# adaLN pieces on VectorE handed out one behind each weight tile's low part, one modulation back on TensorE, one moved into the last SwiGLU

## The chip, the core and the metric

The kernel runs on one core of a Trainium2 chip. Its time is device microseconds (us) of one execution. TensorE (PE in the profile, with its weight loads as PEld) does the matrix products, VectorE (DVE) and ScalarE (ACT) the elementwise work, GpSimd (POOL) a little of it, and SyncE (SP) issues the transfers. Each engine works through its own queue in order and waits there on semaphores.

## What is computed

Two layers over 256 latent and 256 context tokens of width 1024. Every sub-layer is modulated by nine vectors per layer, which come from the conditioning vector by one large product with `w_ada` (the adaLN modulations, number 0 to 8):

```python
m_x = jnp.split((jax.nn.silu(c) @ w_ada[l] + b_ada[l])[:, None, :], N_MOD, axis=-1)
m_c = jnp.split((jax.nn.silu(c_ctx) @ w_ada[l] + b_ada[l])[None, None, :], N_MOD, axis=-1)
x = post_norm(x, 0.5 * m_x[2] * swiglu(modulate(x, m_x[0], m_x[1]), ffn1_wi[l], ffn1_wo[l]), ln_g[l, 0], ln_b[l, 0])
# the same for ctx, then the mixer with m[3..5], then ffn2 with m[6..8]
def swiglu(u, wi, wo):
    gate, up = jnp.split(u @ wi, 2, axis=-1)
    return (jax.nn.silu(gate) * up) @ wo
```

So a layer is SwiGLU (ffn1), mixer, SwiGLU (ffn2). In the last layer ffn2 works on the 256 latent tokens alone.

## The kernel before

**The four SwiGLUs.** `ffn` is called four times; they are called A (layer 0, ffn1), B (layer 0, ffn2), C (layer 1, ffn1) and D (layer 1, ffn2, latent tokens only) below. Each has a first part, the product with `wi`, and a second with `wo`. The first part runs over 22 column blocks m. A block has two weight tiles of 128x1024, gate and up. For each, `wload` issues a 512 KB transfer on SP into `raw` (3 buffers), ScalarE writes the high part `whi` (line 256) and VectorE the low part `wlo` (line 257; 2 buffers of each). `gemm` then runs 24 matmuls a tile, 8 times the three products of lines 266 to 268, the third of which reads `wlo`. After a block, `swiglu` forms `sg` on ScalarE and VectorE (line 420) and splits it into `hh` (ScalarE) and `hl` (VectorE, line 273). In A, B and C the first two blocks run in halves of the tokens while the layer norm ahead of them is ending; block 2 is the first that runs whole.

**The modulations on VectorE.** `ada_pieces` makes one modulation out of nine closures. Eight are pieces: a 512 KB transfer of 128 rows of `w_ada` into `araw` (2 buffers), and two VectorE instructions over 128x1024 that add it, times one column of the conditioning, to the two accumulators (line 192 for the first piece, line 194 for the others). The ninth, the close, sums over the partitions on TensorE (line 199), copies with ScalarE (line 202), transposes on TensorE (line 206) and adds the bias on VectorE (line 208). The accumulators `acc` hold two modulations and have one buffer; the residual `z` of the second part uses the same memory.

**How they are handed out.** `whole` fills the list `bgq` ahead of each `ffn`: six modulations in A, five in B, five in C, none in D. `ffn` traces `nbg` = 3 closures after each block (and after each of the four half blocks at the start), and what is left at the end of the first part. A scheduler then puts the instructions of each engine in an order by its own estimate of when they are ready, so the position in the code sets the order only roughly.

**The modulations on TensorE.** `ada_blocks` makes modulations 0 and 1 of layer 0 at the start of the kernel: for a piece, a 512 KB transfer and four matmuls of 32x256 side by side (line 150); at the end a VectorE copy of the row sums (line 154) and small matmuls with `sel` (line 159).

Of the kernel before, what the change touches and what calls it, by code (L numbers as in the profile page):

```python
# [7 lines left out]
F32 = mybir.dt.float32  # L8
F32R = mybir.dt.float32r
AF = mybir.ActivationFunctionType  # L10
ALU = mybir.AluOpType
# [3 lines left out]
P = 128  # L15
D = 1024
# [5 lines left out]
KF = 22  # L22
# [13 lines left out]
LAT = slice(0, SEQ)  # L36
CTXS = slice(SEQ, NT)
FULL = slice(0, NT)
HALVES = [LAT, CTXS]
# [15 lines left out]
class Program:  # L55
    def __init__(self, tc, A):
        self.tc = tc
        self.nc = tc.nc
        self.A = A
        self.bgq = []  # L60


    def setup(self, ctx):
# [151 lines left out]
    def bg(self, n):  # L215
        while n > 0 and self.bgq:
            self.bgq.pop(0)()
            n -= 1

    def bg_all(self):  # L220
        self.bg(len(self.bgq))

# [20 lines left out]
    def wload(self, src, n, hold=None):  # L243


        nc = self.nc
        raw = self.wp.tile([P, 1024], F32, tag="raw", name="raw", bufs=3)
        nc.sync.dma_start(out=raw[:, :n], in_=src)
        if hold is None:
            hold = [[self.wp.tile([P, 1024], F32R, tag=t, name=t) for t in ("whi", "wlo")]]  # L250
        whs, wls = [], []
        w = 1024 // len(hold)
        for i, (hi, lo) in enumerate(hold):
            r = raw[:, w * i:min(w * i + w, n)]
            m = r.shape[1]
            nc.scalar.activation(out=hi[:, :m], in_=r, func=AF.Copy)  # L256
            nc.vector.tensor_tensor(out=lo[:, :m], in0=r, in1=hi[:, :m].bitcast(F32), op=ALU.subtract)  # L257
            whs += [hi[:, P * k:P * k + P] for k in range(m // P)]
            wls += [lo[:, P * k:P * k + P] for k in range(m // P)]
        return whs, wls  # L260
# [124 lines left out]

        self.ready = [self.wload(s, 1024) for s in srcs]

    def ffn(self, l, which, halves, nxt_fn, nbg, final=None, then=()):
        nc = self.nc
        wi, wo = self.A[which + "_wi"][l], self.A[which + "_wo"][l]  # L390
        ln, gi = (0, 2) if which == "ffn1" else (2, 8)
        self.bd = 0 if which == "ffn1" else 2
        full = slice(halves[0].start, halves[-1].stop)
        with ExitStack() as ctx:
            self.tmp = ctx.enter_context(self.tc.tile_pool(name=f"ft{l}{which}", bufs=2))
            self.abufs = 2
            self.zp = ctx.enter_context(self.tc.tile_pool(name=f"fz{l}{which}", bufs=1))
            self.acc = None
            hp = ctx.enter_context(self.tc.tile_pool(name=f"fh{l}{which}", bufs=KF))
            self.psum(ctx, f"f{l}{which}", mm=6)  # L400
            hh, hl = [], []
            two = len(halves) == 2

            def load(m, held=False):
                ws = []
                for i in range(2):
                    hold = None
                    if held and m > 0:
                        hold = [[hp.tile([P, NT], F32R, tag=t, name="w" + t) for t in ("hh", "hl")] for _ in range(2)]
                    ws.append(self.wload(wi[m, i], 1024, hold=hold))  # L410
                return ws

            def wi_gemm(ps, ws, h):
                for p, w in zip(ps, ws):
                    self.gemm(p[:, h], w, [t[:, h] for t in self.uh], [t[:, h] for t in self.ul])

            def swiglu(pg, pu):
                sg = self.tmp.tile([P, NT], F32, tag="sg", name="sg")
                nc.scalar.activation(out=sg[:, full], in_=pg[:, full], func=AF.Silu)
                nc.vector.tensor_tensor(out=sg[:, full], in0=pu[:, full], in1=sg[:, full], op=ALU.mult)  # L420
                a = hp.tile([P, NT], F32R, tag="hh", name="hh")
                b = hp.tile([P, NT], F32R, tag="hl", name="hl")
                self.split(a[:, full], b[:, full], sg[:, full])
                hh.append(a)
                hl.append(b)

            def banks():
                return [self.bank("mm", [P, NT], n) for n in ("ps_fg", "ps_fu")]


            early = 2 if two else 0
            ps = [banks() for _ in range(early)]
            ready, self.ready = self.ready, []
            ws = [m == 0 and ready or load(m, True) for m in range(early)]
            for h in halves if two else []:
                for m in range(early):
                    wi_gemm(ps[m], ws[m], h)
                    self.bg(nbg)
            for p in ps:
                swiglu(*p)  # L440
            for m in range(early, KF):
                p = banks()
                wi_gemm(p, m == 0 and ready or load(m), full)
                swiglu(*p)
                self.bg(nbg)
            self.bg_all()
            gate = self.gate(l, gi)
            nxt = nxt_fn()
            dst = self.norm_dst(l, ln, nxt, final)
            zt = self.zp.tile([P, KD, NT], F32, tag="z", name="z", bufs=1)  # L450
            self.z = [zt[:, k, :] for k in range(KD)]
            pts = {}

            def wo_gemm(m, h):
                pt = pts[m]
                for a, b in ((0, 8), (8, 15), (15, 22)):
                    w = self.wload(wo[m, :, a:b].rearrange("p k c -> p (k c)"), (b - a) * P)
                    self.gemm(pt[:, h], w, [t[:, h] for t in hh[a:b]], [t[:, h] for t in hl[a:b]], a == 0, b == KF)

            late = 1 if two else 0  # L460
            for m in range(KD):
                pts[m] = self.bank("mm", [P, NT], "ps_o")
                if m < KD - late:
                    xr = self.load_x(m, full)
                    wo_gemm(m, full)
                    for h in halves:
                        self.residual(m, pts[m], xr, h, gate)
                        self.stats_add(m, h)
            for h in halves:
                for m in range(KD - late, KD):  # L470
                    xr = self.load_x(m, h)
                    wo_gemm(m, h)
                    res = self.residual(m, pts[m], xr, h, gate)
                    self.stats_add(m, h)
                if h is not halves[0]:
                    self.ln_norm(l, ln, halves[0], nxt, dst, bc, res)
                if h is halves[-1]:
                    self.make_ready(*then)
                bc = self.ln_stats(h)
            self.ln_norm(l, ln, h, nxt, dst, bc)  # L480
            self.xsrc = dst
# [838 lines left out]
    def whole(self, out):  # L1320
        def wi(l, which):
            return [self.A[which + "_wi"][l, 0, i] for i in range(2)]

        self.start(wi(0, "ffn1"))
        for l in range(DEPTH):
            last = l == DEPTH - 1
            for i in ([2, 3, 4, 5, 6, 7] if l == 0 else [4, 5, 6, 7, 8]):
                self.bgq += self.ada_pieces(l, i)
            self.ffn(l, "ffn1", HALVES, lambda: self.mod_next(l, 3, (l, 0)), 3,
                     then=[self.A["w_in"][l, t] for t in (T_WD, T_AD)])  # L1330
            self.mixer(l, not last, lambda: self.mod_next(l, 6, (l, 1)), wi(l, "ffn2"))
            if not last:
                self.bgq += self.ada_pieces(l, 8)
                for i in range(4):
                    self.bgq += self.ada_pieces(l + 1, i)
                self.ffn(l, "ffn2", HALVES, lambda: self.mod_next(l + 1, 0, (l, 2)), 3, then=wi(l + 1, "ffn1"))
            else:
                self.ffn(l, "ffn2", [LAT], lambda: None, 0, final=out)


def pack(I):
    import numpy as np
    f = np.float32
    A = {}
    xt = np.concatenate([I["x"][0], I["ctx"][0]], 0)
    A["xT"] = xt.T.reshape(KD, P, NT)
    A["cvec"] = np.stack([I["c"][0], I["c_ctx"]], 1).reshape(KD, P, 2).transpose(1, 0, 2)
    A["w_ada0"] = I["w_ada"][0, :, 0:2 * D].reshape(2, 4, P, 2, 4, 256).transpose(3, 4, 0, 2, 1, 5)
    A["w_ada"] = I["w_ada"].reshape(DEPTH, KD, P, 9, D).transpose(0, 3, 1, 2, 4)
    A["bada"] = I["b_ada"].reshape(DEPTH, 9, KD, P).transpose(3, 0, 1, 2)  # L1350
    A["lngb"] = np.stack([I["ln_g"], I["ln_b"]], 2).reshape(DEPTH, 3, 2, KD, P).transpose(4, 0, 1, 2, 3)
# [31 lines left out]
    r = np.arange(SEQ) // GRID_W  # L1383
# [19 lines left out]
    i = np.arange(C)  # L1403
# [30 lines left out]
```

## Time and profile before

| what | value |
|---|---|
| median of 3 runs | 2971.82 us (2965.13 to 2972.13) |
| the profiled execution, its own time | 2964.87 us |
| its span | 2963.1 us |
| busy: PE, PEld, DVE, ACT, POOL | 2806.9, 2237.2, 1779.9, 1069.1, 278.9 us |
| mean granted TensorE clock | 0.965 of full speed |
| VectorE instructions of line 194 (pieces) | 224, 277.2 us |
| DMA, mean over the span | 127 GB/s |

The profiled execution lies 6.95 us under the median and at the low end of the runs; between its span and its time lie 1.8 us. Busy time of PE is modelled: a matmul's record is longer than the distance to the next one, so the distance between starts is what a matmul costs. The granted clock is a share of full speed, and takes one of two levels, 1.2 or 2.4 GHz, at a time. A line in the profile is that of the kernel before, and can be a helper's.

### The profile page before, as it was taken

The page shows a single profiled execution, that of the slowest core. Times are in us where ns is not written, and L with a number is a line of the kernel's source. Part 1 is how long each engine was busy: PE and PEld are TensorE (multiplying, and loading weights), DVE is VectorE, ACT ScalarE, POOL GpSimd, SP SyncE. Part 2 cuts the span into 40 slices and gives each one's busy share as a digit, 9 for nine tenths or more (in the row PEclk, how much of TensorE's full clock was granted, in tenths as well). Part 3 has the DMA queues.
Part 4 walks back from the last instruction along what each step waited for, and adds up shares of the span by engine and source line. Part 5 has one row for each costly group of instructions (what it writes and reads, how often), then busy time and mean ns, then how long its engine had stood idle before and what let it go on. Part 6 is the DMA issues. An engine that isn't in the chain of part 4 may idle for free. (4 is left out here: it accounts for less than half of the span.)

```text
span 2963.1 us, 48510 instructions
## 1 busy us (share of the span) xinstructions
PE 2806.9 (95%) x19598; PEld 2237.2 (76%) x19598; DVE 1779.9 (60%) x3039; ACT 1069.1 (36%) x1929; POOL 278.9 (9%) x274
## 2 busy tenths in 40 slices
PE   7999999999999899998999998999999999898998
PEld 5788887666666776696788876788876677777998
DVE  5983346756674357659832478532568786476554
ACT  3223134323232246442222332222543433364543
POOL 0000011100000111220000110001210100022000
PEclk8999999999999999999999998999999998899998
DMA  7763343221122433346623366433432223354454
GB/s 274 232 221 99 108 137 96 76 68 45 43 59 71 149 104 109 111 139 219 199 94 107 116 206 208 143 97 114 152 107 80 60 64 102 110 138 138 159 179 147
DMA packets 205313, 376.61 MB, mean 127 GB/s; under 512 B 79776, under 2 KB 109088, under 8 KB 205088
## 3 DMA queue, kind: packets, MB, share of 16 engines
q1 hardware_dynamic: 205088, 373.51, 40.7%
q8 instruction: 154, 2.52, 0.3%
q14 instruction: 71, 0.58, 0.1%
HBM read 340.93 MB, written 31.46 MB: 126 GB/s over the span
## 5 line engine op out<-in xcount | busy, mean ns | idle before, releaser
L256 ACT ACTIVATE whi<-raw 128x1024 fp32r<-128x1024 f32 (+1 forms) x399 | 415.2, 1041 | 1072.5 <-PE ps_o L267 305.7
L257 DVE TENSOR_TENSOR wlo<-raw,whi 128x1024 fp32r<-128x1024 f32 (+1 forms) x399 | 500.3, 1255 | 416.5 <-ACT whi L256 410.8
L194 DVE SCALAR_TENSOR_TENSOR acc<-araw,cs,acc 128x1024 f32<-128x1024 f32 x224 | 277.2, 1279 | 28.1 <-DMA araw<-in_w_ada 27.1
L266 PE MATMUL ps_o<-hh,whi 128*128 128x512 f32 (+1 forms) x770 | 270.5, 351 | 0.0
L268 PE MATMUL ps_o<-hh,wlo 128*128 128x512 f32 (+1 forms) x770 | 267.3, 347 | 0.0
L266 PE MATMUL ps_fg<-uh,whi 128*128 128x512 f32 (+1 forms) x704 | 256.8, 365 | 10.2 <-ACT whi L256 6.5
L267 PE MATMUL ps_o<-hl,whi 128*128 128x512 f32 (+1 forms) x770 | 265.5, 345 | 0.0
L268 PE MATMUL ps_fg<-uh,wlo 128*128 128x512 f32 (+1 forms) x704 | 255.2, 362 | 8.5 <-DVE wlo L257 8.5
L268 PE MATMUL ps_fu<-uh,wlo 128*128 128x512 f32 (+1 forms) x704 | 255.3, 363 | 8.2 <-DVE wlo L257 8.2
L762 PE MATMUL ps_gate<-uh,whi 128*128 128x512 f32 (+1 forms) x672 | 255.3, 380 | 3.1 <-ACT whi L256 3.1
L266 PE MATMUL ps_fu<-uh,whi 128*128 128x512 f32 (+1 forms) x704 | 253.8, 361 | 3.1 <-ACT whi L256 3.1
L763 PE MATMUL ps_gate<-ul,whi 128*128 128x512 f32 (+1 forms) x672 | 255.4, 380 | 0.0
L764 PE MATMUL ps_gate<-uh,wlo 128*128 128x512 f32 (+1 forms) x672 | 254.0, 378 | 0.7 <-DVE wlo L257 0.5
L267 PE MATMUL ps_fg<-ul,whi 128*128 128x512 f32 (+1 forms) x704 | 254.4, 361 | 0.1
L267 PE MATMUL ps_fu<-ul,whi 128*128 128x512 f32 (+1 forms) x704 | 253.7, 360 | 0.0
L266 PEld LDWEIGHTS ps_fg<-uh,whi 128*128 128x128 f32 x704 | 135.7, 193 | 39.8 <-ACT whi L256 15.2
L268 PEld LDWEIGHTS ps_o<-hh,wlo 128*128 128x128 f32 x770 | 144.6, 188 | 20.3
L267 PEld LDWEIGHTS ps_o<-hl,whi 128*128 128x128 f32 x770 | 144.5, 188 | 19.6
L268 PEld LDWEIGHTS ps_fg<-uh,wlo 128*128 128x128 f32 x704 | 135.6, 193 | 30.3 <-DVE wlo L257 10.7
L268 PEld LDWEIGHTS ps_fu<-uh,wlo 128*128 128x128 f32 x704 | 135.7, 193 | 30.2 <-DVE wlo L257 11.1
L266 PEld LDWEIGHTS ps_o<-hh,whi 128*128 128x128 f32 x770 | 144.8, 188 | 17.4
L266 PEld LDWEIGHTS ps_fu<-uh,whi 128*128 128x128 f32 x704 | 135.7, 193 | 24.4 <-ACT whi L256 5.6
(298 smaller groups left out, 5268.3 us busy)
## 6 DMA issues: line engine op xcount, KB each, us to landing
raw<-in_ffn_wi SPq DMA_DIRECT2D x176, 512.0 KB, 3.9
araw<-in_w_ada SPq DMA_DIRECT2D x144, 512.0 KB, 4.3
raw<-in_w_in SPq DMA_DIRECT2D x92, 512.0 KB, 3.6
raw<-in_ffn_wo SPq DMA_DIRECT2D x70, 448.0 KB, 3.3
raw<-in_ffn_wo SPq DMA_DIRECT2D x35, 512.0 KB, 3.5
pd<-fg SPq DMA_DIRECT2D x52, 256.0 KB, 2.0
raw<-in_w_branch SPq DMA_DIRECT2D x24, 512.0 KB, 3.7
praw<-in_w_in SPq DMA_DIRECT2D x44, 256.0 KB, 2.8
```

The lines of the kernel that those rows point to most:

```text
L194: nc.vector.scalar_tensor_tensor(out=a, in0=raw, scalar=c, in1=a, op0=ALU.mult, op1=ALU.add)
L256: nc.scalar.activation(out=hi[:, :m], in_=r, func=AF.Copy)
L257: nc.vector.tensor_tensor(out=lo[:, :m], in0=r, in1=hi[:, :m].bitcast(F32), op=ALU.subtract)
L266: nc.tensor.matmul(pt, wh, xh[k], start=first and k == 0, stop=False)
L267: nc.tensor.matmul(pt, wh, xl[k], start=False, stop=False)
L268: nc.tensor.matmul(pt, wl, xh[k], start=False, stop=last and k == n - 1)
L762: nc.tensor.matmul(pt, wh, xh, start=k == 0, stop=False)
L763: nc.tensor.matmul(pt, wh, xl, start=False, stop=False)
L764: nc.tensor.matmul(pt, wl, xh, start=False, stop=k == KD - 1)
```

## The change

Four things. A new method `bg_after` traces closures under `issue_after(self.lo.ins)`: each VectorE instruction among them gets an edge that keeps it behind the last `wlo` instruction in VectorE's queue. `load` calls it with one closure after each weight tile (`every` = 1: after each; 4: after every fourth), and the two half blocks of the context tokens hand out one each; the old three closures after a block are gone. Modulation 2 of layer 0 goes to `ada_blocks`, in eight pieces, one at the end of each of the blocks 2 to 9 of A. Modulation 8 of layer 1 moves from C to D, one closure after every fourth tile.

```diff
+    def bg_after(self, n):
+        with self.tc.issue_after(self.lo.ins):
+            self.bg(n)
...
-            nc.vector.tensor_tensor(out=lo[:, :m], in0=r, in1=hi[:, :m].bitcast(F32), op=ALU.subtract)
+            self.lo = nc.vector.tensor_tensor(out=lo[:, :m], in0=r, in1=hi[:, :m].bitcast(F32), op=ALU.subtract)
...
+            slots = iter(range(2 * KF))
...
                     ws.append(self.wload(wi[m, i], 1024, hold=hold))
+                    if next(slots) % every == 0:
+                        self.bg_after(1)
...
                     wi_gemm(ps[m], ws[m], h)
-                    self.bg(nbg)
+                    if h.start:
+                        self.bg_after(1)
...
                 swiglu(*p)
-                self.bg(nbg)
+                if self.bgpe:
+                    self.bgpe.pop(0)()
...
-            for i in ([2, 3, 4, 5, 6, 7] if l == 0 else [4, 5, 6, 7, 8]):
+            for i in ([3, 4, 5, 6, 7] if l == 0 else [4, 5, 6, 7]):
                 self.bgq += self.ada_pieces(l, i)
-            self.ffn(l, "ffn1", HALVES, lambda: self.mod_next(l, 3, (l, 0)), 3,
+            if l == 0:
+                self.new_mod(0, 2)
+                self.bgpe = self.ada_blocks(0, [2], 0, 4)
+            self.ffn(l, "ffn1", HALVES, lambda: self.mod_next(l, 3, (l, 0)), 1,
...
-                self.ffn(l, "ffn2", [LAT], lambda: None, 0, final=out)
+                self.bgq += self.ada_pieces(l, 8)
+                self.ffn(l, "ffn2", [LAT], lambda: None, 4, final=out)
```

The arrays change in one place: `w_ada0`, the copy of the weights that `ada_blocks` reads, holds three modulations in place of two. New line numbers: pieces 193 and 195, close 200, 203, 207 and 209, `wlo` 263, `sg` 429, `hl` 279, TensorE's pieces 151, row copy 155, `sel` matmuls 160. Outside of the four SwiGLUs no engine's order changes.

**Place 1: VectorE in B, blocks 3 to 5.** Before, from the `sg` of block 2 on (`wlo_11920` is the up tile of block 3, `wlo_12004` and `wlo_12010` are the tiles of block 4):

```order
L420 TENSOR_TENSOR sg_11890<-ps_fu_11829,sg_11890 128x512
L257 TENSOR_TENSOR wlo_11920<-raw_11917,whi_11919 128x1024
L194 SCALAR_TENSOR_TENSOR acc_11614<-araw_11733,cs_71,acc_11614 128x1024 x2
L194 SCALAR_TENSOR_TENSOR acc_11614<-araw_11737,cs_71,acc_11614 128x1024 x2
L273 TENSOR_TENSOR hl_11894<-sg_11890,hh_11893 128x512
L420 TENSOR_TENSOR sg_11971<-ps_fu_11910,sg_11971 128x512
L192 TENSOR_SCALAR acc_11614<-araw_11802,cs_71 128x1024 x2
L208 TENSOR_TENSOR mod0_8_11523<-ps_ada2_11747,c_bada_74 128x8 x2
L273 TENSOR_TENSOR hl_11975<-sg_11971,hh_11974 128x512
L194 SCALAR_TENSOR_TENSOR acc_11614<-araw_11806,cs_71,acc_11614 128x1024 x2
L257 TENSOR_TENSOR wlo_12004<-raw_12001,whi_12003 128x1024
L194 SCALAR_TENSOR_TENSOR acc_11614<-araw_11810,cs_71,acc_11614 128x1024 x2
```

Now, from the same `sg` on (`wlo_11889` is the up tile of block 3, `wlo_11956` and `wlo_11975` are those of block 4):

```order
L429 TENSOR_TENSOR sg_11867<-ps_fu_11798,sg_11867 128x512
L263 TENSOR_TENSOR wlo_11889<-raw_11886,whi_11888 128x1024
L195 SCALAR_TENSOR_TENSOR acc_11566<-araw_11882,cs_71,acc_11566 128x1024
L279 TENSOR_TENSOR hl_11871<-sg_11867,hh_11870 128x512
L195 SCALAR_TENSOR_TENSOR acc_11566<-araw_11882,cs_71,acc_11566 128x1024
L195 SCALAR_TENSOR_TENSOR acc_11566<-araw_11892,cs_71,acc_11566 128x1024 x2
L429 TENSOR_TENSOR sg_11944<-ps_fu_11875,sg_11944 128x512
L263 TENSOR_TENSOR wlo_11956<-raw_11953,whi_11955 128x1024
L279 TENSOR_TENSOR hl_11948<-sg_11944,hh_11947 128x512
L263 TENSOR_TENSOR wlo_11975<-raw_11972,whi_11974 128x1024
L209 TENSOR_TENSOR mod0_8_11533<-ps_ada2_11965,c_bada_74 128x8 x2
L193 TENSOR_SCALAR acc_11566<-araw_11978,cs_71 128x1024 x2
```

Between the up tile of block 3 and the gate tile of block 4 stood four pieces (one of them a first piece), two `hl` and an `sg`; now two pieces, an `hl` and an `sg` stand there.

**Place 2: VectorE in D, one block in the steady part.** Before (gate tile, `sg` of the block ahead, up tile, `hl`):

```order
L257 TENSOR_TENSOR wlo_24928<-raw_24925,whi_24927 128x1024
L420 TENSOR_TENSOR sg_24916<-ps_fu_24855,sg_24916 128x256
L257 TENSOR_TENSOR wlo_24934<-raw_24931,whi_24933 128x1024
L273 TENSOR_TENSOR hl_24920<-sg_24916,hh_24919 128x256
L257 TENSOR_TENSOR wlo_24997<-raw_24994,whi_24996 128x1024
```

Now, in the seven blocks that have a piece so (the other blocks are as before):

```order
L263 TENSOR_TENSOR wlo_24970<-raw_24967,whi_24969 128x1024
L195 SCALAR_TENSOR_TENSOR acc_24690<-araw_24973,cs_71,acc_24690 128x1024
L429 TENSOR_TENSOR sg_24958<-ps_fu_24897,sg_24958 128x256
L195 SCALAR_TENSOR_TENSOR acc_24690<-araw_24973,cs_71,acc_24690 128x1024
L279 TENSOR_TENSOR hl_24962<-sg_24958,hh_24961 128x256
L263 TENSOR_TENSOR wlo_24980<-raw_24977,whi_24979 128x1024
```

The two instructions of a piece stand on both sides of `sg`, and the up tile's `wlo` has moved behind the second and behind `hl`.

**Place 3: TensorE in A, from a block's last matmul into the next.** Before, at a close:

```order
L268 MATMUL ps_fu_1233<-uh_93,wlo_1243 128x512
L199 MATMUL ps_ada_1309<-acc_888,one_82 32x512 x4
L266 MATMUL ps_fg_1322<-uh_86,whi_1326 128x512
L267 MATMUL ps_fg_1322<-ul_94,whi_1326 128x512
L268 MATMUL ps_fg_1322<-uh_86,wlo_1327 128x512
L266 MATMUL ps_fg_1322<-uh_87,whi_1326 128x512
L267 MATMUL ps_fg_1322<-ul_95,whi_1326 128x512
L206 MATMUL ps_ada2_1315<-c_ident_78,acc_888 128x128 x4
L268 MATMUL ps_fg_1322<-uh_87,wlo_1327 128x512
```

Now, at the end of block 9, with the last piece of modulation 2 and its `sel` matmuls, four matmuls later (`rows_1289` is VectorE's copy, which stands behind the `sg` of block 9 there):

```order
L274 MATMUL ps_fu_1206<-uh_93,wlo_1221 128x512
L151 MATMUL ps_ada_682<-araw_1283,cs_71 32x256 x4
L272 MATMUL ps_fg_1295<-uh_86,whi_1299 128x512
L273 MATMUL ps_fg_1295<-ul_94,whi_1299 128x512
L274 MATMUL ps_fg_1295<-uh_86,wlo_1300 128x512
L272 MATMUL ps_fg_1295<-uh_87,whi_1299 128x512
L160 MATMUL ps_ada2_1291<-c_sel_69,rows_1289 128x8 x2
L273 MATMUL ps_fg_1295<-ul_95,whi_1299 128x512
```

Each of the eight pieces (`L151`, four matmuls) stands so between two blocks, and `L160` waits on VectorE in the midst of block 10.

## Rows read from the trace of the kernel before

**Rows 1.** The page's second part: busy tenths of VectorE in 40 slices.

```profile
DVE  5983346756674357659832478532568786476554
```

**Rows 2.** Waits of TensorE over the whole span: total us, times, longest.

```profile
PE ps_fg L268 <- DVE wlo L257: 8.5, 6, 5.5
PE ps_fu L268 <- DVE wlo L257: 8.2, 4, 3.9
```

**Rows 3.** Ten microseconds of B: window, length, busy of PE, PEld, DVE, ACT, POOL, clock, DMA.

```profile
1350.00:1360.00 10.00, 4.11 (x22) 2.01 (x21) 9.00 (x13) 2.17 (x3) 0.00 (x0) 0.86 0.57 166
```

**Rows 4.** VectorE's order of time, B without pieces: start, us, instruction, idle before.

```profile
1486.58 0.69 DVE L420 TENSOR_TENSOR sg<-ps_fu,sg 128x512 f32<-128x512 f32 x1 [3.37 <-PE ps_fu L268]
1497.46 0.69 DVE L420 TENSOR_TENSOR sg<-ps_fu,sg 128x512 f32<-128x512 f32 x1 [3.37 <-PE ps_fu L268]
```

**Rows 5.** TensorE's order of time: first matmul of block 2, first behind block 21.

```profile
64.00 0.40 PE L266 MATMUL ps_fg<-uh,whi 128*128 128x512 f32 x1
...
300.52 0.40 PE L266 MATMUL ps_o<-hh,whi 128*128 128x512 f32 x1
...
1326.87 0.40 PE L266 MATMUL ps_fg<-uh,whi 128*128 128x512 f32 x1
...
1573.35 0.40 PE L266 MATMUL ps_o<-hh,whi 128*128 128x512 f32 x1
...
1734.39 0.40 PE L266 MATMUL ps_fg<-uh,whi 128*128 128x512 f32 x1
...
1982.25 0.40 PE L266 MATMUL ps_o<-hh,whi 128*128 128x512 f32 x1
```

**Rows 6.** TensorE's order of time at a close in A.

```profile
130.30 0.39 PE L268 MATMUL ps_fu<-uh,wlo 128*128 128x512 f32 x1
130.62 1.07 PE L199 MATMUL ps_ada<-acc,one 128*32 128x512 f32 x8
...
133.01 0.48 PE L267 MATMUL ps_fg<-ul,whi 128*128 128x512 f32 x1
```

**Rows 7.** VectorE, then TensorE, in B at blocks 3 and 4; TensorE in C.

```profile
1346.94 4.87 DVE L194 SCALAR_TENSOR_TENSOR acc<-araw,cs,acc 128x1024 f32<-128x1024 f32 x4 [0.74 <-DMA araw<-in_w_ada]
...
1358.58 1.22 DVE L257 TENSOR_TENSOR wlo<-raw,whi 128x1024 fp32r<-128x1024 f32 x1
...
1351.91 1.06 PE L199 MATMUL ps_ada<-acc,one 128*32 128x512 f32 x8 [0.34 <-issue]
...
1359.85 0.79 PE L268 MATMUL ps_fg<-uh,wlo 128*128 128x512 f32 x1 [5.51 <-DVE wlo L257]
...
1759.37 0.50 PE L268 MATMUL ps_fg<-uh,wlo 128*128 128x512 f32 x1 [1.23 <-DVE wlo L257]
```

**Rows 8.** The tile `araw`: a piece's instruction (ns), and its transfer (us to landing).

```profile
L194 DVE SCALAR_TENSOR_TENSOR acc<-araw,cs,acc x224: 1272/1279/1287, 49.1 to 1880.1; 128x1024 f32<-128x1024 f32 x112
...
DMA to landing us min/median/max: 3.4/4.3/10.0
```

**Rows 9.** TensorE's order of time at the kernel's start (modulations 0 and 1).

```profile
9.82 1.08 PE L150 MATMUL ps_ada<-araw,cs 128*32 128x256 f32 x8 [0.20 <-DMA araw<-in_w_ada]
...
20.46 0.61 PE L159 MATMUL ps_ada<-c_sel,rows 128*128 128x8 f32 x4 [1.60 <-DVE rows L154]
...
21.87 3.26 PE L150 MATMUL ps_ada<-araw,cs 128*32 128x256 f32 x32
```

**Rows 10.** VectorE, then TensorE, in one block of D.

```profile
2840.10 1.23 DVE L257 TENSOR_TENSOR wlo<-raw,whi 128x1024 fp32r<-128x1024 f32 x1 [1.37 <-ACT whi L256]
2842.03 0.42 DVE L420 TENSOR_TENSOR sg<-ps_fu,sg 128x256 f32<-128x256 f32 x1 [0.70 <-PE ps_fu L268]
2842.93 1.23 DVE L257 TENSOR_TENSOR wlo<-raw,whi 128x1024 fp32r<-128x1024 f32 x1 [0.47 <-ACT whi L256]
...
2845.86 1.22 DVE L257 TENSOR_TENSOR wlo<-raw,whi 128x1024 fp32r<-128x1024 f32 x1 [1.37 <-ACT whi L256]
...
2844.88 0.28 PE L268 MATMUL ps_fu<-uh,wlo 128*128 128x256 f32 x1
```

More of the change, by code (lines that the diff above doesn't have):

```diff
@@ L60, in __init__ @@
         self.bgq = []
+        self.bgpe = []
     def setup(self, ctx):
@@ L386, in make_ready, with ffn @@
         self.ready = [self.wload(s, 1024) for s in srcs]
-    def ffn(self, l, which, halves, nxt_fn, nbg, final=None, then=()):
+    def ffn(self, l, which, halves, nxt_fn, every, final=None, then=()):
         nc = self.nc
@@ L1335, in whole @@
                     self.bgq += self.ada_pieces(l + 1, i)
-                self.ffn(l, "ffn2", HALVES, lambda: self.mod_next(l + 1, 0, (l, 2)), 3, then=wi(l + 1, "ffn1"))
+                self.ffn(l, "ffn2", HALVES, lambda: self.mod_next(l + 1, 0, (l, 2)), 1, then=wi(l + 1, "ffn1"))
             else:
-                self.ffn(l, "ffn2", [LAT], lambda: None, 0, final=out)
+                self.bgq += self.ada_pieces(l, 8)
+                self.ffn(l, "ffn2", [LAT], lambda: None, 4, final=out)
 def pack(I):
@@ L1347, in pack @@
     A["cvec"] = np.stack([I["c"][0], I["c_ctx"]], 1).reshape(KD, P, 2).transpose(1, 0, 2)
-    A["w_ada0"] = I["w_ada"][0, :, 0:2 * D].reshape(2, 4, P, 2, 4, 256).transpose(3, 4, 0, 2, 1, 5)
+    A["w_ada0"] = I["w_ada"][0, :, 0:3 * D].reshape(2, 4, P, 3, 4, 256).transpose(3, 4, 0, 2, 1, 5)
     A["w_ada"] = I["w_ada"].reshape(DEPTH, KD, P, 9, D).transpose(0, 3, 1, 2, 4)
```

## The prediction

> **What bounds the kernel now.** I read the page's slices first, then the waits of TensorE, then the order of time of TensorE and VectorE in each SwiGLU. The slices say where VectorE is full: its nines stand where the pieces are handed out, most of all in B and C [rows 1], although over the whole span it is not the busiest engine. The waits say who suffers: TensorE waits for `wlo`, ten times, 16.7 us in all [rows 2]. That is less than what is lost, because the granted clock falls behind a long wait: in the ten microseconds of B around the wait of 5.51 us TensorE is busy for 4.11 us and has a mean clock of 0.86, while VectorE works for 9.00 [rows 3, 7]. Of the two levels, 1.2 and 2.4 GHz, part of that window ran at the lower.
>
> To size the whole loss I compare the length of 20 blocks (2 to 21) with what they take when nothing is in the way. In B behind the last piece two `sg` of neighbouring blocks stand 1497.46 − 1486.58 = 10.88 us apart, with TensorE the releaser and VectorE idle for 3.37 us [rows 4], so 20 blocks at full speed are 217.6. They took 236.5 in A, 246.5 in B and 247.9 in C [rows 5]. A close costs TensorE the distance between the matmuls around it less five spacings: (133.01 − 130.30) − 5 × 0.227 = 1.58 us [rows 6]. With six, five and five closes the losses are 236.5 − 217.6 − 9.5 = 9.4 in A, 246.5 − 217.6 − 7.9 = 21.0 in B and 22.4 in C. Some 53 us is thus the most that a perfect order could give back in A, B and C without changing the work.
>
> Why it is lost: three closures a block are 3 × 2.48 = 7.4 us of VectorE (a pair of instructions; one is 1.28 [rows 7, 8]: four in a row took 4.87). With two `wlo` at 1.22 and `sg` and `hl` at about 0.69 each [rows 4, 7] the block wants 7.4 + 2.45 + 1.38 = 11.3 us of VectorE, more than TensorE's 10.88. And the pieces bunch up: in B four instructions stood ahead of the `wlo` that ran at 1358.58, and TensorE got its matmul at 1359.85 [rows 7].
>
> **What the change removes in B and C.** Two pieces a block are 4.96 + 2.45 + 1.38 = 8.8 us, 2.1 below 10.88; and one `wlo` has at most one piece, an `sg` and an `hl` ahead of it: 2.5 + 0.7 + 0.7 + its own 1.2 = 5.1 us. A tile lasts 5.44 us on TensorE, so a `wlo` whose queue empties one tile ahead is ready. So the waits should go once the new order has begun. It doesn't begin at once: up to 1351.91 in B, and up to the wait ahead of 1759.37 in C, the instructions stand much as before. By then two blocks have taken 1351.91 − 1326.87 = 25.0 us in B and (1759.37 − 0.45) − 1734.39 = 24.5 in C [rows 5, 7] instead of 21.8, so 3.3 and 2.8 of the losses stay.
>
> B: of 21.0 the first 3.3 stays, and I leave as much again, 3.3, for a close whose transposes wait for VectorE and for a dip of the clock: −14.4 (from −9, if half of what follows the first two blocks stays, to −21). C: of 22.4 the first 2.8 stays and the rest goes, −19.6, and it has one close less, −1.6: −21.2 (from −12 to −24).
>
> **What it adds in A.** Modulation 2 leaves VectorE and one close with it (−1.58), and adds eight pieces on TensorE. A piece is four matmuls of 32x256 side by side. The nearest rows: at the start of the kernel, where the pieces of two modulations go together, eight records of 32x256 take 1.08 and thirty-two 3.26, and the eight of 32x512 in a close take 1.07 [rows 6, 9]. Four are then 0.41 (an eighth of 3.26) at the least, 0.54 by half of a group of eight, and 1.08 at the most, if a group costs the same whatever is in it. I take 0.65, nearest to the half group: 8 × 0.65 = 5.2 (3.3 to 8.6). In the close, the first matmul starts 0.32 behind the one ahead of it, not 0.227 [rows 6], so part of the cost, 0.09 going in and something like it coming out, does not shrink with the columns; that is why I stay above 0.54. The Trainium skill ("TensorEngine Tiling (Array Packing)", Key Properties) says that a change of the tiling mode drains TensorE, which speaks against eight small groups between full matmuls. The row agrees, with 0.09 us; by the rule the eight pieces would cost about 1 us more than half groups, which lies inside my bounds.
>
> Then the `sel` matmuls, 0.6 [rows 9], and ahead of them a stall. TensorE reaches them about 0.9 us into block 10, but they read a VectorE copy that stands behind the `sg` of block 9. In these blocks `araw` has three users and two buffers: the tied piece behind the gate tile, the one behind the up tile and TensorE's own. A transfer lands 4.3 us after its issue (3.4 to 10.0) [rows 8]. The up tile's piece can issue only when a buffer is free, and the one behind it lands another 4.3 later, so VectorE stands at a piece with `sg` and the copy queued behind it until some 3.7 us into block 10. So 3.7 − 0.9 = 2.8 (0, if the buffers come free earlier, to 5). The Trainium skill ("DMA: Bandwidth & Descriptors", Anatomy of one DMA) fits a transfer on GpSimd's path as 2.0 us plus bytes over 436 GB/s, an estimate of 3.2 us for 512 KB. The row of this kernel's SP transfers says 4.3, and the measurement decides; by the fit the stall would be about 0.6, and the whole sum 2.2 us lower.
>
> The loss of 9.4 goes with VectorE's load, as in B. A then is 217.6 + 5 × 1.58 + 5.2 + 0.6 + 2.8 = 234.1 against 236.5: −2.4 (−6 with the low ends; +4 if a third of the loss stays, and more under rival 1).
>
> **What it adds in D.** D is half as wide, its block is 2845.86 − 2840.10 = 5.76 us [rows 10], and had no pieces. Per block VectorE has 2.45 + 0.42 and a narrow `hl`, so its time is there: a piece of 2.5 every second block fits. Its place does not. In the row's block the gate `wlo` ends at 2841.3; now a half piece runs to 2842.6, `sg` follows, which ran at 2842.03 before, then the second half and `hl`, and the up tile's `wlo`, which ended at 2842.93 + 1.23 = 2844.16, ends at about 2845.9: 2842.6 + 0.42 + 1.28 + 0.4 (an `hl` as wide as that `sg`) + 1.22. TensorE wants it at 2844.76, its matmul starting at 2844.88 [rows 10]. The slack of 0.6 to 0.7 is thus overdrawn by about 1.05. Seven blocks have this place: 7 × 1.05 = 7.4, and the close adds 1.6: **+9.0** (0, where the blocks that follow absorb it through a `wlo` that is ready early, to 15 with twice the wait). The nine transfers issue on SP between those of the weights. With 1 MB of weights per block and half a MB per two, D would move about 230 GB/s; 166 GB/s took 0.57 of the DMA engines [rows 3], so 230 would take about 0.8: they fit, which hides them, and if that cover is gone each late tile would show as a wait for `whi`.
>
> **The sum.** −2.4 − 14.4 − 21.2 + 9.0 = −29.0. Against the profiled execution, 2964.87, that is 2935.9. The median lies 6.95 higher, so from there it is 2942.8. I forecast 2939, between the two. By the ends of the terms the sum goes from −6 − 21 − 24 + 0 = −51 to +4 − 9 − 12 + 15 = −2; ends that do not fall together give about 2927 to 2952.
>
> **Rivals.** (1) *The ties turn into waits for `araw`.* VectorE takes its queue in order, so a piece that stands right behind one `wlo` and waits for its transfer holds up `sg`, `hl` and the next `wlo`. With two users the two buffers give a transfer 10.88 − 2.5 = 8.4 us, and 4.3 is the median, so B and C hold; in A's blocks 2 to 9 there are three users. If each of those eight blocks loses 1 to 1.5 us, A costs 8 to 12 more: about 2949. For it: the longest landing is 10.0 [rows 8].
>
> (2) *More goes than I say*: the early stalls of B and C go too (6), the remainder I left in B (3), and D's wait is hidden (7): 2939 − 16 = 2923. Against it: the early orders hardly change.
>
> (3) *Slower: D falls to the low clock.* A wait of 5.51 us in B brought the clock to 0.86 in its window [rows 3]. If D's repeated waits do the same for the stretch of 14 blocks that holds its pieces, each block can take up to 5.76 more; all fourteen are +80, 3019. From five such blocks (29 / 5.76) nothing is left, from seven the kernel is slower by more than a measurement tells from no change, which here is about 0.3%, or 9 us. Against it: a wait is about 1 us, not 5.5; and at the low clock a block is so long that the wait is gone.
>
> (4) *The gain is given back, or the change doesn't do what it says*: the waits for `wlo` pass to another engine's product, as the 0.69 or 1.37 us that lie behind ScalarE's `whi` in places, or VectorE bunches pieces in spite of the ties. Half of B's and C's gains gone and D at its high end: −29 + 18 + 6 = −5, about 2964. Against it: the new order shows single pieces between the `wlo`.
>
> **Chances.** Forecast 0.64, rival 1 0.13, rival 2 0.09, rival 3 0.05, rival 4 0.09. The forecast with rivals 1 and 2 and part of the unknown ends asks for 2920 to 2957. Faster by over 0.3% (below 2962.9) is the forecast, rivals 1 and 2, less their tails: 0.82; within 0.3% rival 4 and a tail: 0.11; slower rival 3 and a tail: 0.07.
>
> **What would show it.** In B and C: no wait of TensorE for `wlo` behind block 4, a pitch of 10.88, the clock at 1.00. In A: one wait for the row copy near block 10, eight groups of four small matmuls at some 0.65 each. In D: seven waits for `wlo` of about 1 us. It is wrong if VectorE shows idle time before pieces, released by `araw`'s transfers, in B or C, or if D's blocks grow by more than their wait.

## The result, and the profile after

The changed kernel takes 2939.68 us (median of four runs, 2933.89 to 2944.01) against 2969.51 (four runs) of the kernel before: a ratio of 0.990, interval 0.9875 to 0.9924. The forecast was 2939. The profiled execution took 2933.89, its span 2932.1; against the profiled execution of before that is 31.0 us less, where the sum said 29.0.

The first matmul of block 2 and the first behind block 21, in A, B and C (TensorE's order of time, after; the same places as [rows 5]):

```profile
65.18 0.40 PE L272 MATMUL ps_fg<-uh,whi 128*128 128x512 f32 x1
...
298.25 0.51 PE L272 MATMUL ps_o<-hh,whi 128*128 128x512 f32 x1
...
1326.18 0.40 PE L272 MATMUL ps_fg<-uh,whi 128*128 128x512 f32 x1
...
1554.78 0.51 PE L272 MATMUL ps_o<-hh,whi 128*128 128x512 f32 x1
...
1715.38 0.40 PE L272 MATMUL ps_fg<-uh,whi 128*128 128x512 f32 x1
...
1943.27 0.40 PE L272 MATMUL ps_o<-hh,whi 128*128 128x512 f32 x1
```

A took 233.1 (236.5 before), B 228.6 (246.5), C 227.9 (247.9). D, from block 2 to its end, took 122.7 (115.2): see below. The four differences are −3.5, −17.9, −20.0 and +7.5, −33.8 together; the stretches between them were 2.8 longer, 1.2 of it ahead of A's block 2, and −31.0 is left.

TensorE's waits for `wlo` over the span, after (total us, times, longest; [rows 2] were 8.5 and 8.2):

```profile
PE ps_fu L274 <- DVE wlo L263: 5.1, 8, 1.6
PE ps_fg L274 <- DVE wlo L263: 1.7, 3, 0.7
```

The closes waited too, for the accumulators that VectorE had not finished (TensorE's waits, before and after). The prediction did not list these:

```profile
PE ps_ada L199 <- DVE acc L194: 8.0, 6, 2.9
...
PE ps_ada L200 <- DVE acc L195: 1.6, 2, 1.3
```

Where these waits went is seen best by stretches. First before: B from block 2 to 1417.62, B behind that up to the close of the last piece, C from block 2 to 1860.66 (window, length, busy of PE, PEld, DVE, ACT, POOL, clock, DMA share, GB/s):

```profile
1326.87:1417.62 90.75, 76.91 (x326) 57.44 (x325) 82.23 (x88) 19.85 (x26) 0.00 (x0) 0.94 0.69 224
1417.62:1474.83 57.21, 57.21 (x262) 45.49 (x260) 50.09 (x53) 17.78 (x23) 0.00 (x0) 1.00 0.65 214
1734.39:1860.66 126.27, 113.50 (x482) 86.63 (x481) 110.21 (x118) 30.17 (x39) 0.00 (x0) 0.93 0.69 220
```

The VectorE instructions of the pieces alone (the tile `araw`, two to a piece) in the first two of these windows, before:

```profile
1326.87:1417.62 90.75, 0.00 (x0) 0.00 (x0) 61.55 (x54) 0.94 0.69 224
1417.62:1474.83 57.21, 0.00 (x0) 0.00 (x0) 31.99 (x27) 1.00 0.65 214
```

After, the first four blocks or so of B, the rest of B, and the same of C:

```profile
1326.18:1369.08 42.90, 40.96 (x182) 31.73 (x181) 37.47 (x40) 10.59 (x14) 0.00 (x0) 1.00 0.72 232
1369.08:1554.78 185.70, 185.70 (x837) 150.08 (x835) 129.54 (x136) 55.29 (x71) 0.00 (x0) 1.00 0.54 172
1715.38:1764.12 48.74, 45.99 (x206) 36.31 (x205) 40.80 (x45) 12.38 (x17) 0.00 (x0) 1.00 0.69 227
1764.12:1943.27 179.15, 179.15 (x806) 145.58 (x804) 107.13 (x115) 52.70 (x68) 0.00 (x0) 1.00 0.47 149
```

Two things are to be seen. After, TensorE is busy for the whole of the long windows, at a clock of 1.00; what is left of the loss, some 3 us in B and in C, lies in the first blocks. And before, all of B's loss lay in the *first six* blocks: 90.75 us for 6 × 10.88 + 3 closes, 65.3 + 5.1, so 20.4 too many (a close counts 1.69 here: its block is 1.08 longer than 10.88 and the next 0.61), of which 13.8 is idle (90.75 − 76.91) and the other 6.6 slower work, at a mean clock of 0.94. In these six blocks stand 54 instructions, 27 pieces or 4.5 a block: just what the twelve closures of the half blocks and three behind each block make (30, three of them closes). VectorE had 82.23 us of work there, where TensorE at full speed needs 70.4. Behind 1417.62 it had 2.6 pieces a block (13.5 in 57.21 us), was busy for 50.09 of 57.21, and TensorE lost nothing. These rows stood in the trace of before, and the prediction had not read them.

### The profile page after: what moved, and what is told of

Same layout as the page of the kernel before. It is cut to its first block, busy times and chain, and to the rows that moved or that the text cites. A ratio compares the mean times of both kernels' runs of the same rounds, so it can differ in the third digit from the quotient of the medians.

```text
span 2932.1 us, 48565 instructions
## 1 busy us (share of the span) xinstructions
PE 2795.4 (95%) x19654; PEld 2229.4 (76%) x19654; DVE 1766.0 (60%) x3023; ACT 1068.6 (36%) x1928; POOL 277.6 (9%) x274
## 5 line engine op out<-in xcount | busy, mean ns | idle before, releaser
L195 DVE SCALAR_TENSOR_TENSOR acc<-araw,cs,acc 128x1024 f32<-128x1024 f32 x210 | 260.6, 1279 | 14.3 <-DMA araw<-in_w_ada 14.0
L272 PEld LDWEIGHTS ps_o<-hh,whi 128*128 128x128 f32 x770 | 144.7, 188 | 20.4 <-ACT whi L262 1.7
L773 PEld LDWEIGHTS ps_gate<-uh,whi 128*128 128x128 f32 x672 | 130.2, 194 | 28.3 <-issue 5.7
```

The lines of the kernel that those rows point to most:

```text
L195: nc.vector.scalar_tensor_tensor(out=a, in0=raw, scalar=c, in1=a, op0=ALU.mult, op1=ALU.add)
L272: nc.tensor.matmul(pt, wh, xh[k], start=first and k == 0, stop=False)
L773: nc.tensor.matmul(pt, wh, xh, start=k == 0, stop=False)
```

## The experiments

Executions of one kernel differ by up to 30 us (the kernel before ran between 2957.60 and 2987.92 in one set of runs, the changed kernel, run again, between 2924.72 and 2946.01), much more than the 0.3% at which the prediction meant to tell a change from none. In the profiles the difference lies for the most part between the four SwiGLUs and not in them: the stretch from C's end to D's block 2 was 780.9 to 790.3 long in kernels that differ only in D or in C's last closures. So a verdict of a few us rests on the stage lengths, which repeat better. Four to six kernels each share the changed kernel's code of a stage; they gave 232.1 to 233.4 in A, 228.5 to 230.3 in B, 226.0 to 229.7 in C and 122.65 to 122.70 in D. A smaller difference than that spread tells nothing. All lengths are from the first matmul of block 2 to the first behind block 21, one profile each, and each ratio is to runs of the kernel before that were timed beside the kernel:

| kernel | A | B | C | D | median us | ratio to before, interval |
|---|---|---|---|---|---|---|
| before | 236.5 | 246.5 | 247.9 | 115.2 | 2969.51 | |
| the change | 233.1 | 228.6 | 227.9 | 122.7 | 2939.68 | 0.9900 (0.9875 to 0.9924) |
| the change again | 232.1 | 230.0 | 226.7 | 122.7 | 2938.82 | 0.9876 (0.9847 to 0.9905) |
| untied | 236.7 | 228.7 | 226.5 | 119.1 | 2933.73 | 0.9872 (0.9841 to 0.9904) |
| before, two a block | 229.9 | 239.5 | 233.2 | 115.2 | 2940.21 | 0.9889 (0.9858 to 0.9921) |
| pairs | 232.1 | 234.1 | 228.9 | 122.7 | 2930.22 | 0.9841 (0.9801 to 0.9880) |
| before, three but late | 235.4 | 233.7 | 235.2 | 115.2 | 2937.19 | 0.9873 (0.9839 to 0.9907) |
| D behind the up tile | 233.3 | 228.5 | 229.7 | 120.4 | 2938.22 | 0.9888 (0.9861 to 0.9914) |
| D in halves | 233.4 | 230.3 | 226.0 | 117.9 | 2931.86 | 0.9867 (0.9834 to 0.9901) |
| modulation 8 in C | 233.3 | 229.9 | 229.5 | 115.2 | 2930.56 | 0.9855 (0.9811 to 0.9898) |
| modulation 2 on VectorE | 225.5 | 228.7 | 228.6 | 122.7 | 2929.76 | 0.9850 (0.9815 to 0.9885) |
| halves, late start | 231.2 | 225.7 | 227.6 | 117.2 | 2927.10 | 0.9843 (0.9802 to 0.9885) |
| combined | 229.1 | 230.7 | 225.9 | 117.7 | 2924.19 | 0.9819 (0.9787 to 0.9850) |
| combined, from block 3 | 229.0 | 226.6 | 224.4 | 117.2 | 2916.40 | 0.9803 (0.9778 to 0.9828) |

**Is it the place or the rate?** First the tie alone is undone:

```diff
-        with self.tc.issue_after(self.lo.ins):
-            self.bg(n)
+        self.bg(n)
```

> The changed kernel with the edge to the low part of the weight tile left out: the closures are traced at the same places and in the same number, but the scheduler orders VectorE by its own estimate. In its order two and a half pieces stand together ahead of a low part in most blocks of B and C. Theory 'place' (the gain comes from no low part having more than one piece ahead of it): the waits of TensorE for `wlo` come back in B and C, together 10 to 25 us slower than the changed kernel, 2950 to 2965. Theory 'rate' (the gain comes from two pieces a block in place of three): within 4 us of the changed kernel.

B and C are as short as in the change (228.7 and 226.5). The theory "place" is wrong: the edge gives nothing in B and C. It is worth 3.6 us in A, where an untied close waits 2.33 us for its accumulators and the `sel` matmuls 0.66 for their copy, and costs as much in D (119.1 against 122.7).

Next the rate alone, in the kernel before:

```diff
-            ... lambda: self.mod_next(l, 3, (l, 0)), 3,
+            ... lambda: self.mod_next(l, 3, (l, 0)), 2,
```

(and so in B.)

> The kernel before with two closures after a block in place of three; nothing tied, modulation 2 on VectorE, modulation 8 of layer 1 in C. Theory 'rate': B and C fall to about 230 us each for blocks 2 to 21 and D stays at 115.2, so about 2933. Theory 'place': pieces still stand two and three together, B and C keep a good half of their 21 and 22 us, so 2950 to 2965.

Neither theory has it right. C falls by 14.6 us and B by 7.0 only, and most of B's rest is one wait, in the same place as that of [rows 7], and the lower clock behind it; from the block after the next on, nearly every block is 10.9 us beside the closes:

```profile
1360.30 0.79 PE L268 MATMUL ps_fg<-uh,wlo 128*128 128x512 f32 x1 [5.77 <-DVE wlo L257]
```

What the two kernels share is the heap of closures traced in the half blocks, eight here, twelve before, two in the change (with two more behind the tiles of block 1). So a third theory: the heap at the start. It was taken away alone, with the rate of three kept:

```diff
                     wi_gemm(ps[m], ws[m], h)
-                    self.bg(nbg)
+                    if h.start:
+                        self.bg(1)
```

> The kernel before with three closures after a block as before, but in the four half blocks at the start of A, B and C only one behind each of the two context halves (two in place of twelve). Theory 'the heap at the start': with the twelve gone the long blocks of B and C (14 to 20 us where 10.9 is the full speed) shrink to 10.9 beside the closes, B and C 226 to 232, total about 2935. Theory 'the rate of three': 11.3 us of VectorE a block against 10.88 lets it fall behind by 0.4 a block whatever the start, long blocks stay up to the last piece, B and C 236 to 245, total 2950 to 2962.

B falls by 12.8 and C by 12.7 of the 17.9 and 20.0 that the change gives (18.3 in C without the close that the change moved out of it). It lies between the two expectations: the heap alone makes about seven tenths of the gain. The parts do not simply add up, since two a block with a heap of eight gave 7.0 in B but 14.6 in C. What is left at three a block has another look: waits of about 1 us, and no lower clock: B up to 1500 has 1.00. (In C one of them, 1.72 us, is a close whose transposes wait for ScalarE's copy.) VectorE runs without a gap from 1403.70 to 1414.4, and one and a half pieces and an `hl` stand ahead of a `wlo`. But just ahead of that run it had stood 1.65 us for a piece's transfer, and 1.90 us at the same place ahead of the second wait shown. Whether the rate alone makes these waits, or the two `araw` buffers with it, no run tells (VectorE in B, then TensorE, which waits for that `wlo` and for one like it later):

```profile
1403.70 2.48 DVE L194 SCALAR_TENSOR_TENSOR acc<-araw,cs,acc 128x1024 f32<-128x1024 f32 x2 [1.65 <-DMA araw<-in_w_ada]
...
1408.43 0.68 DVE L420 TENSOR_TENSOR sg<-ps_fu,sg 128x512 f32<-128x512 f32 x1
1409.03 1.28 DVE L194 SCALAR_TENSOR_TENSOR acc<-araw,cs,acc 128x1024 f32<-128x1024 f32 x1
1410.22 0.68 DVE L273 TENSOR_TENSOR hl<-sg,hh 128x512 fp32r<-128x512 f32 x1
1410.83 2.47 DVE L194 SCALAR_TENSOR_TENSOR acc<-araw,cs,acc 128x1024 f32<-128x1024 f32 x2
1413.22 1.22 DVE L257 TENSOR_TENSOR wlo<-raw,whi 128x1024 fp32r<-128x1024 f32 x1
```

```profile
1414.49 0.50 PE L268 MATMUL ps_fu<-uh,wlo 128*128 128x512 f32 x1 [0.76 <-DVE wlo L257]
...
1486.90 0.50 PE L268 MATMUL ps_fu<-uh,wlo 128*128 128x512 f32 x1 [1.09 <-DVE wlo L257]
```

At two a block, does the spacing matter? Both closures behind the up tile, none behind the gate tile:

```diff
-                    if next(slots) % every == 0:
-                        self.bg_after(1)
+                    k = next(slots)
+                    if every == 1:
+                        if k % 2:
+                            self.bg_after(2)
+                    elif k % every == 0:
+                        self.bg_after(1)
```

> The changed kernel with the same number of closures a block in A, B and C and the same edge, but both behind the up tile's low part, none behind the gate tile's. Theory 'even spacing matters beside the rate': two pieces, 5 us, stand ahead of the next gate tile's low part, which comes 0.5 to 2 us late in most blocks; B and C 235 to 245 each, total 2950 to 2970. Theory 'the rate alone': B and C stay at 228, total unchanged.

No, not where VectorE has time: C stays at 228.9, and in the steady part of B two pieces, 4.86 us, stand ahead of the gate tile's low part and TensorE waits for nothing (VectorE, one block; no wait of TensorE lies between 1368 and 1396):

```profile
1374.46 1.23 DVE L263 TENSOR_TENSOR wlo<-raw,whi 128x1024 fp32r<-128x1024 f32 x1
1375.61 0.68 DVE L279 TENSOR_TENSOR hl<-sg,hh 128x512 fp32r<-128x512 f32 x1
1376.21 4.86 DVE L195 SCALAR_TENSOR_TENSOR acc<-araw,cs,acc 128x1024 f32<-128x1024 f32 x4
1380.99 1.21 DVE L263 TENSOR_TENSOR wlo<-raw,whi 128x1024 fp32r<-128x1024 f32 x1
1384.55 0.69 DVE L433 TENSOR_TENSOR sg<-ps_fu,sg 128x512 f32<-128x512 f32 x1 [2.34 <-PE ps_fu L274]
```

VectorE idles 2.3 us a block there, and that slack takes this order too. B's 5.5 us more are one wait of 3.66 us in block 3 with the lower clock behind it (0.79 from 1338 to 1344). The wait at this place was 0.2 to 1.8 us in the kernels with the change's B, and 3.68 in one of those below without pairs, so it says little of the spacing; its cause was not tested here.

**D.** In the change six blocks have the same wait. VectorE, then TensorE, in one of them (the place of [rows 10]):

```profile
2733.59 1.28 DVE L195 SCALAR_TENSOR_TENSOR acc<-araw,cs,acc 128x1024 f32<-128x1024 f32 x1
2734.78 0.42 DVE L429 TENSOR_TENSOR sg<-ps_fu,sg 128x256 f32<-128x256 f32 x1
2735.12 1.28 DVE L195 SCALAR_TENSOR_TENSOR acc<-araw,cs,acc 128x1024 f32<-128x1024 f32 x1
2736.31 0.42 DVE L279 TENSOR_TENSOR hl<-sg,hh 128x256 fp32r<-128x256 f32 x1
2736.65 1.22 DVE L263 TENSOR_TENSOR wlo<-raw,whi 128x1024 fp32r<-128x1024 f32 x1
```

```profile
2737.11 0.28 PE L273 MATMUL ps_fu<-ul,whi 128*128 128x256 f32 x1
2737.92 0.39 PE L274 MATMUL ps_fu<-uh,wlo 128*128 128x256 f32 x1 [0.54 <-DVE wlo L263]
```

Two kernels move only D's pieces: behind the up tile, and cut in two closures of one instruction each, one behind every gate tile.

```diff
-                    if next(slots) % every == 0:
+                    if next(slots) % every == every // 4:
```

> The changed kernel with D's closures behind the up tile's low part in place of the gate tile's. In D's order a whole piece then stands behind `hl`, ahead of the next gate tile's low part. Theory 'a whole piece fits in no gap of D': the wait of about 0.54 us moves from the up tile to the gate tile, D stays at 121 to 124 us for blocks 2 to 21, total within 2 us of the changed kernel. Theory 'the gate tile's place is the fault': D falls to 117, total about 6 us lower.

```diff
-                self.bgq += self.ada_pieces(l, 8)
-                self.ffn(l, "ffn2", [LAT], lambda: None, 4, final=out)
+                self.bgq += self.ada_pieces(l, 8, True)
+                self.ffn(l, "ffn2", [LAT], lambda: None, 2, final=out)
```

> The changed kernel with D's pieces cut in two closures, one VectorE instruction each, one behind each gate tile's low part (16 halves and a close). Theory 'a whole piece fits in no gap of D, half of one does': no wait for `wlo` in D, D is 115.2 + 1.7 = 117 us, total 5 to 6 us below the changed kernel, about 2934. Theory 'any VectorE work or transfer in D costs': D stays near 122 and the total is unchanged.

Behind the up tile the six waits stay but are 0.15 us each, 120.4; halves have a single wait of 0.51, 117.9. Half a piece fits D's gaps and a whole one does not, and transfers have nothing to do with it: D moved 213 GB/s in halves, 204 in the change. What is left of D's cost, some 2 us, is the close.

Or D is left alone and modulation 8 stays in C:

```diff
-            for i in ([3, 4, 5, 6, 7] if l == 0 else [4, 5, 6, 7]):
+            for i in ([3, 4, 5, 6, 7] if l == 0 else [4, 5, 6, 7, 8]):
```

> The changed kernel with modulation 8 of layer 1 back in C, on VectorE like the others, D without pieces. Theory 'C had room': D is 115.2 us for blocks 2 to 21 (122.7 in the changed kernel), C takes one close more, 229 to 231 (227.9), total 4 to 6 us below the changed kernel. Theory 'moving it out of C is what freed C': C goes back by 5 us or more and the total is the same or higher.

D is 115.2. C is 229.5, at the upper end of its spread, as one close more would have it. C had room: moving the modulation into D was no part of the gain.

**A.** Modulation 2 goes back to VectorE:

```diff
-            for i in ([3, 4, 5, 6, 7] if l == 0 else [4, 5, 6, 7]):
+            for i in ([2, 3, 4, 5, 6, 7] if l == 0 else [4, 5, 6, 7]):
...
-                self.bgpe = self.ada_blocks(0, [2], 0, 4)
```

> The changed kernel with modulation 2 of layer 0 on VectorE again, nine closures more in A, all tied; the ten that find no tile are left to the end of A's first part. Theory 'TensorE pays more for the eight pieces than VectorE would': A's blocks 2 to 21 fall by 4 to 7 us to 226 to 229, the leftovers fit beside the product with `wo`, and the total falls by 3 to 6. Theory 'VectorE is full': the leftovers hold up the weights of `wo` and the total is 0 to 10 us higher.

A's first part is 225.5, 7.6 shorter. The ten closures left over cost about 4 of that in the product with `wo` (TensorE's rows there):

```profile
298.28 0.50 PE L274 MATMUL ps_o<-hh,wlo 128*128 128x512 f32 x1 [1.05 <-DVE wlo L263]
...
311.16 1.06 PE L200 MATMUL ps_ada<-acc,one 128*32 128x512 f32 x8 [0.69 <-DVE acc L195]
```

From block 2 to A's last `ps_o` matmul it is 356.7 against 360.4 in the change (and 363.4 before). So TensorE paid some 3.6 us more for the modulation than VectorE would have, by one profile of each; the last two kernels below, with the modulation on VectorE, have an A of 229.

**Together.** First D in halves and no closure in the half blocks; then modulation 2 on VectorE too, with a second closure behind every fourth tile of A so that nothing is left; then in B and C no closure ahead of block 3:

```diff
-                    if h.start:
-                        self.bg_after(1)
```

> The kernel with D's pieces in halves, and with no closure handed out in the half blocks at the start of A, B and C (two fewer each, left to the end of the first part). Theory 'the early stalls come from the closures at the half blocks': the waits in blocks 2 to 4 of B and C shrink, B and C 226 each, total about 4 us below the kernel with halves alone. Theory 'they come from the layer norm before': B and C unchanged within 1 us, the leftovers cost 0 to 2 us.

```diff
+                    if h.start and (l, which) == (0, "ffn1"):
...
+                        self.bg_after(1 + ((l, which) == (0, "ffn1") and k % 4 == 3))
```

> All that the runs so far point to: modulation 2 on VectorE, with a second closure behind every fourth tile in A so that nothing is left over; no closure in the half blocks of B and C; D's pieces in halves. By the stage lengths of the single runs: A with the product behind it 4 to 6 below the changed kernel, B 3 below, C the same, D 5 below; 12 to 14 us below the changed kernel, about 2926. If the second closure in A is too much for VectorE, long blocks show in A and the total stays above 2930.

```diff
+                    if k % every == 0 and (k >= 4 or not two or (l, which) == (0, "ffn1")):
+                        self.bg_after(1 + (l == 0 and two and k % 4 == 3))
```

> The combined kernel with the first closure of B and C behind the third block's gate tile (no piece is traced before), and in B a second closure behind every fourth tile as in A. Theory 'what stays of the early waits is the heap of pieces traced in the first blocks': no wait for `wlo` and no block over 12 in B and C, B 225 to 226, C 224 to 225, total 3 to 5 us below the combined kernel, about 2920. Theory 'the layer norm before them is what is late': blocks 2 to 4 stay long and the total is unchanged.

The first is undecided for C: it shortened B (225.7), but C kept waits of 1.08 and 1.52 us. The second kept, with the same order, one wait of 3.68 us in B's block 3 behind four piece instructions, which is 0.24 in the kernel of the first: TensorE came 3 us sooner this time, and the pieces, which stood 2.7 us for their transfers, ended no sooner. With the third, which has no pieces there, all waits for `wlo` in A, B and C are gone, and the clock is 1.00 throughout:

```profile
1321.89:1548.51 226.62, 226.23 (x1022) 182.60 (x1021) 165.61 (x176) 65.86 (x85) 0.00 (x0) 1.00 0.60 185
1707.90:1932.32 224.42, 224.42 (x1011) 182.13 (x1009) 148.61 (x161) 64.99 (x84) 0.00 (x0) 1.00 0.55 170
```

The gain is C's, 224.4; B's 226.6 is no shorter than the first's. The kernel takes 2916.40 and is the fastest; timed beside the same runs of before, its ratio of 0.9803 (0.9778 to 0.9828) lies clear of the change's 0.9876 (0.9847 to 0.9905).

> The changed kernel once more, for a comparison with the two combined kernels beside the same runs of the kernel before: 2936 to 2944, a ratio of 0.99 to the kernel before; its stages A to D within 2 us of the first profile, if stage lengths tell more than totals.

## Why the prediction was right, and which of its steps were not

**The sum.** The terms were −2.4, −14.4, −21.2 and +9.0 and came out as −3.5, −17.9, −20.0 and +7.5. Each lies within its own bounds. Together they are −33.8, 4.8 more than the sum; that the profiled executions came within 2 us of it (31.0 against 29.0) is due to the stretches between the stages, 2.8 us longer in this one execution, and is luck.

**Why it was lost: the step that failed.** The prediction had VectorE as the one that is late, which is right, but put it down to the rate and the order: three closures a block want 11.3 us of VectorE, more than 10.88, and a low part should have at most one piece ahead. It counted three closures as three pieces, but one in nine is a close: 3 × 8/9 × 2.48 = 6.6, with 2.45 + 1.38 10.4 us a block on the mean. That fits, barely, as the window behind 1417.62 shows, and still leaves single waits, as the kernel with three but late shows. And two pieces ahead of a low part cost nothing in the steady part at two a block. About seven tenths of the gain came from the heap of the half blocks, which made 4.5 pieces a block out of 2.7 in B's first six blocks. The prediction passed over it: it listed these closures in the kernel, and never priced them. The sum came out all the same, since it was taken from the lengths of 20 blocks and not from the cause. What it left in B for later closes and dips, 3.3 us, was not lost; the 3.3 and 2.8 kept for the first blocks were (3.1 in B and 3.5 in C, with a close at 1.69).

**A.** The total was near, its parts were not. A piece costs 0.78 to 0.80, not 0.65: eight are some 6.3. The stall ahead of the `sel` matmuls, put at 2.8, is not there: VectorE copies at 162.84, just behind `sg`, and TensorE goes on without a wait (TensorE's rows, the piece of another block and then the `sel` matmuls):

```profile
112.22 0.39 PE L274 MATMUL ps_fu<-uh,wlo 128*128 128x512 f32 x1
112.54 0.64 PE L151 MATMUL ps_ada<-araw,cs 128*32 128x256 f32 x8
113.11 0.50 PE L272 MATMUL ps_fg<-uh,whi 128*128 128x512 f32 x1
113.45 0.39 PE L273 MATMUL ps_fg<-ul,whi 128*128 128x512 f32 x1
...
163.66 0.51 PE L160 MATMUL ps_ada<-c_sel,rows 128*128 128x8 f32 x4
```

The price of a piece had been read with a slip: eight records were taken for the pieces of two modulations and halved, but a matmul of this form leaves two records (the kernel before has 128 of them for 64 matmuls), so eight are one piece. At a granted clock of 0.50 they take 1.08 (the same line at 29.39 us, before, in a window at that clock), at 1.00 they take 0.64:

```profile
29.39 1.08 PE L150 MATMUL ps_ada<-araw,cs 128*32 128x256 f32 x8
...
29.39:30.47 1.08, 1.08 (x13) 0.60 (x16) 0.33 (x2) 0.52 (x2) 0.00 (x0) 0.50 1.04 393
```

From the row ahead to the second behind it is 113.45 − 112.22 = 1.23; less two spacings of 0.227 that is 0.78. Of that the way in (0.32) and out (0.34) take 0.2 more than plain spacings. The Trainium skill ("TensorEngine Tiling (Array Packing)", Key Properties) says that a change of the tiling mode drains TensorE; the trace agrees, with 0.2 us a piece, twice what the prediction saw on the way in alone.

**D.** The mechanism and the place were right, and also that short waits leave the clock: 1.00 through the rows of D. The wait was mis-sized: six blocks of 0.79 (0.54 of wait and the slower restart, 2737.92 − 2737.11 = 0.81 for 0.12) and not seven of 1.05; the close and its neighbours cost 2.75 in place of 1.6, its matmuls being split over two places here.

**The rivals.** (1) In A, while TensorE was in blocks 6 and 7, VectorE did stand for `araw`, four times for 1.25 to 2.43 us, but TensorE lost by it no more than 1.26 us ahead of one close. (2) The early stalls stayed. (3) D's clock did not fall. (4) The waits did not pass to `whi`. Two signs that the prediction had named for being wrong did show, in small: D's blocks grew by more than their wait (0.79 for 0.54), and VectorE idled 3.23 us for a piece's transfer in C's block 2, ahead of C's waits of 1.64 and 0.75 us:

```profile
1717.83 1.42 DVE L193 TENSOR_SCALAR acc<-araw,cs 128x1024 f32<-128x1024 f32 x2 [3.23 <-DMA araw<-in_w_ada]
```

## What to carry to other kernels

When side work is handed out evenly, look at what is handed out before the even part begins: here a heap of twelve closures at the start of a stage made more than half of the loss, and five later blocks of the same trace took the same rate without a loss. Where an engine has about a fifth of a block to spare, as VectorE in the steady part of B and C, spacing and ties gained nothing; where it has gaps of half a piece, as in D, cut the piece. And side work is dearer on the engine that sets the pace, as the eight pieces on TensorE were, than on one with time to spare.

## What was not expected of the hardware

A wait costs more than its length where TensorE comes back at the lower level behind it. In the first six blocks of B before, 6.6 us of slower work stood beside 13.8 of idle time: behind the wait of 5.51 us the clock was 0.50 from 1361 to 1363 and 1.00 from 1366 on. Single waits of 2.9 to 5.8 us in B and C were followed by the lower level, while waits of 0.5 to 1.6 us, six in a row 12 us apart in D or four within a stage, left it at 1.00. The length of one wait does not decide it, though. In A before, three waits of 0.81, 1.73 and 0.70 us within 6 us brought the clock to 0.50, and in the kernel with three but late a close that waited 2.72 us (at 101.44) left it at 1.00 (A before, then that kernel):

```profile
74.00:80.00 6.00, 5.30 (x20) 3.56 (x13) 4.88 (x8) 0.60 (x1) 0.00 (x0) 0.50 0.69 221
...
101.44:113.00 11.56, 11.56 (x53) 9.66 (x54) 5.86 (x13) 3.09 (x4) 0.00 (x0) 1.00 0.57 175
```
